# A two-layer trunk on one core: square root of the last norm on ScalarE, and a planner that counts TensorE's instruction transfers

## The chip, the cores and the metric

The kernel runs on one core of one Trainium2 chip. The metric is device time in microseconds, the median of several executions. Beside it there is one profiled execution, whose trace gives the time of every instruction; "span" is the time from its first to its last instruction.

## The reference

The kernel computes a trunk of two layers on x (1 x 256 x 1024, float32) with 256 memory tokens. Every layer is a SwiGLU block, a mixer with memory cross-attention beside it, and a second SwiGLU block, each behind a residual and a layer norm:

```python
for i in range(DEPTH):
    x = layer_norm(ALPHA * x + 0.5 * swiglu(x, ffn1_w_gate[i], ffn1_w_up[i], ffn1_w_down[i]), ...)
    ...
    heads = jnp.concatenate([mix, memory_attention(mq, mem_k, mem_v)], axis=-1)
    x = layer_norm(ALPHA * x + heads @ w_out[i], ...)
    x = layer_norm(ALPHA * x + 0.5 * swiglu(x, ffn2_w_gate[i], ffn2_w_up[i], ffn2_w_down[i]), ...)
```

with `swiglu(x) = (silu(x @ w_gate) * (x @ w_up)) @ w_down`, widths 1024 to 2816 to 1024. Layer 0's mixer is an RWKV-7 recurrence over 12 heads of 64, layer 1's is stick-breaking attention. The layer norm is

```python
return ((xf - mu) * lax.rsqrt(var + LN_EPS) * g + b).astype(x.dtype)
```

## The kernel before, in words

The 256 rows of x are two halves of 128 partitions. All weights are streamed from HBM once, in blocks (tiles `raw`), mainly over SP's queue, some issued from ScalarE. For most large products a weight block is split by ScalarE and VectorE into a rounded part (`hi`) and the rest (`lo`); x and the hidden activations (`hT`) are split the same way, and TensorE multiplies hi by hi, lo by hi and hi by lo in f32r, three 128x512 matmuls where native float32 would take one in two passes. Some blocks are multiplied unsplit in native float32 (`raw` as an operand of a matmul). Layer 0's recurrence is worked in chunks of 64 rows, as many small 64x64 products in native float32 (the tiles `Y`, `T`, `Tt`, `Lm`, `L`, `S`, `vn`, `Sk`, `kn`, `qr` in the rows below); each of these stands as two matmuls in the trace. These small products fall around 250 to 285 us and 400 to 430 us, between large products of the projections, which fill the waits of the recurrence. `ps_N` are banks of PSUM.

The order of the work is not that of the code. The class `Plan` records every operation as an `Op` with its engine and what it depends on (`add`), gives it a duration by shape (`price`), and plays a list scheduler over the five engines (`order`): at each step the free operation with the best urgency is placed, buffers of a tag and, where an operation may run on either ScalarE or VectorE, its engine are chosen, and the model keeps account of semaphores, table loads of ScalarE (`SETS` lists the functions that share a table) and TensorE's clock window (`WINDOW`). `improve` takes each operation's urgency from `URGENCY`, a packed table of numbers, one for each operation in the order of recording. `issue` then writes out all instructions in that order, so that every instruction has one and the same line in the profile: L767 before, L788 after the change. Each engine runs its own instructions strictly in the written order.

`layer_norm` computes one half's norm on VectorE: the residual is added, then bn_stats and bn_aggr give mean and variance (`mv[:, 0:2]`), a `tensor_scalar` gives −(var + eps)/2 in `mv[:, 3:4]`, and `rsqrt` finds the inverse root in `mv[:, 2:3]` from an integer shift (a second `tensor_scalar`) and three Newton rounds of two `scalar_tensor_tensor` each, with a scratch tile of the tag `nw`. Every piece of x then takes two operations, one that subtracts the mean and multiplies by g, and one that multiplies by the inverse root and adds b. `closing` is set for the very last norm of the program (half 1 of layer 1), which works in pieces of 512, 256 and 256 columns; behind each piece its output DMA is issued.

Of the kernel before, what the change touches and what calls it, by code (L numbers as in the profile page):

```python
# [23 lines left out]
P = 128  # L24
# [48 lines left out]
FLAGS = dict(t1=False, bt=False, dc=False, out1=False, zl2=False, pb=False, xt=False, mn=False, tn=False, vn=False)  # L73
# [40 lines left out]
class Op:  # L114
    __slots__ = ("i", "eng", "calls", "took", "lag", "after", "opens", "closes", "pri", "func", "port", "left", "ready",
                 "end", "users", "kb", "turns", "mode", "share", "spent", "fine", "parts", "round", "places", "ways")


class Engine_:
# [7 lines left out]
SETS = (("Exp", "Tanh"), ("Sigmoid", "Tanh"), ("Ln",), ("Silu", "Tanh"))  # L127
# [3 lines left out]
WINDOW = 3413.0  # L131
ROUNDS = 50
# [3 lines left out]
    'c-l?edDu=>)Iad^B%+Y1P)Q;s6=fbmL?lCo43#-UGDb2Kp(0~4&lJi~B2qFWDnq778YLo%l9KT3-)Fz~dtLAEkLS9Fv(MgZeb;w=*V^Zt`>FG32;'  # L136
    'DOz$(YPZa^&9-K1@rJwg3C~|G)2T%nwPDq@4=kY488JDoO72I{vaGS$!#lSw8>i^Wncjc;RFS<DGLbYwGxd%abIhV<&%4ec$EkBzfF-YySMd&yV@'
    'M>W|dtZaGq)i<eE3Hm5^qa7~hY^Gygl%(wHu5PsSjLeq>%@`%4B=5K%b|GnPl-0=rO$bLnVJj$mf{vI&r4Q#x^_+8Q03nBFLdg|^ZnXxZ~D&~FPy'
    'p^&f$$78y&W5n!$|PwEk3xBq<jo@?{Cb=D92?D^`>#)uedpP=J!S8j>`9XGVhH!1PJMpTeE*p1bN=OL)2(cqb8C_m>6#>4#)i-?6KwBHlD*Dpx+R'
    '3~*j(!S5H{YJBp>}6!rb%_?sWb;=6VON$NV*b`-JPv!=9;ZZ^Q0~ehZ-)zw+IXBu)4<%wHz{KE<}K#&luFmDV0mAW1s?9K!C0lVtPc5OTIjl6qf+'  # L140
    'aBN2i#lE)weMvI^E-`*Jgu*qG<X+zuGXJ^GN%CO9B>CIt*R5S;eF%95C&`{gA!IbZ>=HH^b2WRHR!fp~FNKh+gn3ql@b^t{5%2fl*u4}VHiR&ft('
    'Eg6NkOkWDksU)+fw+nHtxdBNm3u)bIak)<`AZx3*ldLjgLGy9KsP;oq$`lTax5qz8vkFB-eEb;T9OoESV(3jk^MdpRwz&A8`;C2R6dmoa<npOi7Z'
    '=14H-)Kd-KuBoE<M^O+(1$*-&458=h8NwT<QlH^(zLT>ym3e!LLgs>e)3KU9`x$@-6{7G_|c(tx0SIk-as}MSe5a$0A!rfvu@}m%Lo5{ZEAzTZ$o'
    'P4O`c*8OL+MFbHCx)=<l_c4=B7_c;tb<2Oe=!zUbK%_ZoJo=oFLsqrk`go0lDqn3LzpvR!M$lohQ8_Hs%@9T)-t#wo@W{)N!E(|U!Nqimxr(%*D~'
    '?tCpdI1oFu<-dBQVEGS=FgaNtMW-Ebm=+u?JHALWaMFyxxFWHOFyY!pISb7sZk_V_dMSO`7X{rR;?GV0MJx#!yu?!t$XzI%m@C1BH<&)<G0M&fwh'
    'Yj!a_$DgCK#T>uxy@zgy*%{oaAO>y4bU&WFg>z5do+KUK;YYO)t{01U#J6}a`68}oa6POJ;SDj(^(LQ=hA_i=@6v#Q@}o7shv3<Pen~QJaR{eimz'
    '7QBehOg<9Z3_%+ed{^>Q#Il7s4~n&CRD~rITb6j0>I#VH;oH!L2dIt*hwxt`H`Rc{8!T*Vrn?mYW2??df4aWBOs8p13g@*Oz&pzLHK_r`^Nwe>O>'
# [140 lines left out]
class Plan:  # L288
# [217 lines left out]
    def order(self, given=()):  # L506
# [1386 lines left out]
```

## Time and profile before

| | us |
|---|---|
| median of 3 executions | 1061.63 (1060.88 to 1062.44) |
| the profiled execution | 1061.31 |
| its span | 1059.5 |
| mean clock granted to TensorE | 0.994 of full speed |
| TensorE busy | 1041.7 |
| VectorE busy | 883.6 |
| ScalarE busy | 740.9 |

How it is read: PE is TensorE, PEld its weight loads, DVE VectorE, ACT ScalarE, POOL GpSimd and SP SyncE. A list of waits puts each idle time of an engine down to the operation that came last among those awaited; "issue" stands where nothing that the profile shows was awaited. A row of a timeline is start, duration, engine, line, operation, output<-inputs, tile sizes, count, and in brackets the idle time ahead of it. A row of a table of stretches is the stretch, its length, the busy time (and instruction count) of PE, PEld, DVE, ACT and POOL, TensorE's granted clock, the DMA engines' share and GB/s. Buffer numbers in names tell which buffer of a tag the operation got.

### The profile page before, as it was taken

What the parts mean: (1) busy time and instruction counts of PE and PEld (TensorE: products, weight loads), DVE (VectorE), ACT (ScalarE), POOL (GpSimd) and SP (SyncE); (2) the same over time, 40 slices, a digit from 0 to 9 for tenths busy, and PEclk for the clock granted to TensorE, in tenths of its full rate; (3) what the DMA queues carried; (4) which work ended last, traced back from release to release, by engine and by line L of the source; (5) the groups of instructions that cost most, each with busy time, mean ns of one, the idle gap of its engine ahead of it and who ended that gap; (6) DMA issues with size and microseconds to landing.
All of it is one profiled execution on the core that took longest, in us unless ns stands there. A gap on an engine that the chain in (4) does not pass through costs nothing.

```text
span 1059.5 us, 17849 instructions
## 1 busy us (share of the span) xinstructions
PE 1041.7 (98%) x6275; PEld 835.5 (79%) x6275; DVE 883.6 (83%) x1241; ACT 740.9 (70%) x1065; POOL 5.3 (0%) x20
## 2 busy tenths in 40 slices
PE   9999999999899999999999999999999999999996
PEld 7888888877688776688888888888778777878885
DVE  6676679999899997898799755469899999976688
ACT  6665559968689887667677544457987998865572
POOL 0000000000000000000000000000000000000000
PEclk9999999999899999999999999999999999999998
DMA  9997869779399788799899966677989989997891
GB/s 327 329 369 242 270 215 352 247 253 336 115 338 328 255 264 290 242 339 329 284 340 366 325 211 215 193 255 254 370 297 313 364 285 304 368 349 258 276 311 67
DMA packets 212684, 303.19 MB, mean 286 GB/s; under 512 B 13892, under 2 KB 159728, under 8 KB 212594
## 3 DMA queue, kind: packets, MB, share of 16 engines
q1 hardware_dynamic: 212050, 301.53, 85.5%
q8 instruction: 49, 0.80, 0.3%
q10 hardware_dynamic: 544, 0.52, 0.2%
q14 instruction: 41, 0.34, 0.1%
HBM read 300.95 MB, written 1.05 MB: 285 GB/s over the span
## 4 chain that ended last, share of the span: by engine, by line
PE 97%; DVE 1%; ACT 1%; DMA 0%; issue 0%; SPq 0%; DVEq 0%; ACTq 0%
PE ps_29r L767 30%; PE ps_30r L767 28%; PE ps_27r L767 8%; PE ps_26r L767 8%; PE ps_3r L767 8%; PE ps_25r L767 8%; PE ps_5r L767 4%; PE ps_6r L767 3%; DMA raw_12r<-in_ffn_w_up_dram 0%; DVE x L767 0%; DVE L_345r L767 0%; SPq L767 0%; ACT hi_10r L767 0%; ACT Lm_333r L767 0%; DVE lo_11r L767 0%
## 5 line engine op out<-in xcount | busy, mean ns | idle before, releaser
L767 PE MATMUL ps_29r<-hi_13r,xTh 128*128 128x512 f32 x64 | 26.3, 411 | 0.0
L767 PE MATMUL ps_29r<-hi_43r,xTh 128*128 128x512 f32 x64 | 26.0, 406 | 0.0
L767 PE MATMUL ps_29r<-lo_14r,xTh 128*128 128x512 f32 x66 | 25.8, 390 | 0.0
L767 ACT ACTIVATE idle_2r<-ps_29r 128x256 f32<-128x256 f32 (+1 forms) x31 | 12.8, 411 | 18.4 <-PE ps_29r L767 18.3
L767 PE MATMUL ps_29r<-hi_46r,xTh 128*128 128x512 f32 x62 | 25.1, 405 | 0.0
L767 PE MATMUL ps_29r<-hi_43r,xTl 128*128 128x512 f32 x64 | 25.1, 392 | 0.0
L767 PE MATMUL ps_29r<-hi_13r,xTl 128*128 128x512 f32 x64 | 25.0, 391 | 0.0
L767 PE MATMUL ps_29r<-hi_46r,xTl 128*128 128x512 f32 x62 | 24.2, 390 | 0.0
L767 PE MATMUL ps_29r<-lo_44r,xTh 128*128 128x512 f32 (+1 forms) x62 | 23.8, 383 | 0.0
L767 PE MATMUL ps_30r<-lo_11r,xTh 128*128 128x512 f32 (+1 forms) x62 | 23.8, 383 | 0.0
L767 PE MATMUL ps_29r<-lo_11r,xTh 128*128 128x512 f32 x58 | 22.8, 392 | 0.7 <-DVE lo_11r L767 0.7
L767 PE MATMUL ps_30r<-hi_46r,xTh 128*128 128x512 f32 (+1 forms) x58 | 23.0, 396 | 0.0
L767 PE MATMUL ps_29r<-hi_7r,xTh 128*128 128x512 f32 x54 | 22.6, 419 | 0.1
L767 PE MATMUL ps_30r<-lo_17r,xTh 128*128 128x512 f32 x58 | 22.6, 390 | 0.0
L767 PE MATMUL ps_29r<-lo_8r,xTh 128*128 128x512 f32 x58 | 22.6, 390 | 0.0
L767 PE MATMUL ps_29r<-lo_17r,xTh 128*128 128x512 f32 x58 | 22.6, 390 | 0.0
L767 PE MATMUL ps_30r<-lo_47r,xTh 128*128 128x512 f32 x58 | 22.6, 390 | 0.0
L767 PE MATMUL ps_30r<-hi_46r,xTl 128*128 128x512 f32 (+1 forms) x58 | 22.2, 383 | 0.0
L767 PE MATMUL ps_30r<-hi_22r,xTh 128*128 128x512 f32 x54 | 22.1, 410 | 0.0
L767 PE MATMUL ps_29r<-hi_16r,xTh 128*128 128x512 f32 x54 | 22.1, 409 | 0.0
L767 PE MATMUL ps_30r<-hi_10r,xTh 128*128 128x512 f32 x54 | 22.1, 409 | 0.0
L767 PE MATMUL ps_29r<-lo_47r,xTh 128*128 128x512 f32 x56 | 21.8, 390 | 0.0
(2125 smaller groups left out, 3922.4 us busy)
## 6 DMA issues: line engine op xcount, KB each, us to landing
raw_21r<-in_ffn_w_down_dram SPq DMA_DIRECT2D x19, 512.0 KB, 5.4
raw_67r<-in_ffn_w_gate_dram SPq DMA_DIRECT2D x32, 256.0 KB, 5.8
raw_67r<-in_ffn_w_up_dram SPq DMA_DIRECT2D x32, 256.0 KB, 6.0
raw_15r<-in_ffn_w_down_dram SPq DMA_DIRECT2D x16, 512.0 KB, 6.0
raw_12r<-in_ffn_w_gate_dram SPq DMA_DIRECT2D x31, 256.0 KB, 4.0
raw_12r<-in_ffn_w_up_dram SPq DMA_DIRECT2D x31, 256.0 KB, 4.6
raw_45r<-in_ffn_w_gate_dram SPq DMA_DIRECT2D x31, 256.0 KB, 6.3
raw_45r<-in_ffn_w_up_dram SPq DMA_DIRECT2D x31, 256.0 KB, 5.5
```

The source lines that it names most:

```text
L767: fn(*[at(x) for x in a], **{n: at(x) for n, x in k.items()})
```

## The change

It has three parts. `price` counts TensorE's instructions of each operation, and `order` moves a position `issued` along TensorE's instruction stream; where it crosses an edge (the first at 94.7, then every 127.1 counted matmuls) less than 5500 ns after the last crossing, the scheduler's model adds the difference to the operation's modelled time. `URGENCY` is replaced by another table (the old one without, the new one with these edges). And the closing norm takes its inverse root another way: a first square root of a constant, due behind the last silu, stands for the load of the table; a second one takes sqrt(var + eps) on ScalarE; VectorE takes its reciprocal and one Newton round (`polish`).

```diff
-FLAGS = dict(..., vn=False)
+FLAGS = dict(..., vn=False, sq=True)
...
-SETS = (("Exp", "Tanh"), ("Sigmoid", "Tanh"), ("Ln",), ("Silu", "Tanh"))
+SETS = (("Exp", "Tanh"), ("Sigmoid", "Tanh"), ("Ln",), ("Silu", "Tanh"), ("Sqrt",))
...
+FETCH = 5500.0
+CHUNK = 127.1
+CHUNK0 = 94.7
...
 URGENCY = (
...
@@ price
+            o.count += 1 if method == "transpose" or st.dtype == F32R else 2
...
@@ order
+        issued, edge, crossed = 0, CHUNK0, -FETCH
...
+                first, took_, stall = issued, took, 0.0
+                issued += o.count
+                while issued > edge:
+                    at_ = t + stall + took_ * (edge - first) / o.count
+                    if at_ < crossed + FETCH:
+                        stall += crossed + FETCH - at_
+                        at_ = crossed + FETCH
+                    crossed = at_
+                    edge += CHUNK
+                took = took_ + stall
...
+    def polish(dst, a, t):
+
+        nc.vector.scalar_tensor_tensor(t, dst, dst, a, ALU.mult, ALU.mult)
+        nc.vector.scalar_tensor_tensor(dst, t, 1.5, dst, ALU.add, ALU.mult)
...
@@ layer_norm
-        rsqrt(mv[:, 2:3], mv[:, 3:4], 1)
+        if FLAGS["sq"] and closing:
+            sd = new(tp_, [P, NH], F32, "nw", "sd", 2)
+            first = nc.scalar.activation(sd[:, 1:2], ident[:, :1], AF.Sqrt)
+            first.after.append(max(o.i for o in nc.ops if o.func in ("Silu", "Tanh")))
+            nc.scalar.activation(sd[:, :1], mv[:, 3:4], AF.Sqrt, scale=-2.0)
+            nc.vector.reciprocal(mv[:, 2:3], sd[:, :1])
+            polish(mv[:, 2:3], mv[:, 3:4], sd[:, 2:3])
+        else:
+            rsqrt(mv[:, 2:3], mv[:, 3:4], 1)
```

The new table moves operations on all engines by a few places; the number of TensorE's rows (4592) stays. Three places are shown as the order has them, before and after, without row numbers.

The first is TensorE in the first stretch of small products of the recurrence: three groups of 24 products (Y·T, T·Y and Tt·Lm) with large 128x512 products around them. Before:

```order
L767 MATMUL ps_30r<-hi_22r,lo_11r 128x512
L767 MATMUL ps_29r<-hi_40r,hi_7r 128x512
L767 MATMUL ps_29r<-lo_41r,hi_7r 128x512
L767 MATMUL ps_29r<-hi_40r,lo_47r 128x512
L767 MATMUL ps_26r<-Y_340r,T_339r 64x64 x2
...
L767 MATMUL ps_25r<-T_339r,Y_340r 64x64 x2
...
L767 MATMUL ps_26r<-Tt_332r,Lm_333r 64x64 x2
...
L767 MATMUL ps_29r<-hi_16r,hi_7r 128x512
```

After:

```order
L788 MATMUL ps_29r<-hi_65r,lo_11r 128x512
L788 MATMUL ps_25r<-Y_340r,T_339r 64x64 x2
...
L788 MATMUL ps_26r<-T_339r,Y_340r 64x64 x2
...
L788 MATMUL ps_29r<-hi_40r,hi_46r 128x512
L788 MATMUL ps_29r<-lo_8r,hi_46r 128x512
L788 MATMUL ps_29r<-hi_40r,lo_11r 128x512
L788 MATMUL ps_29r<-hi_40r,hi_46r 128x512
L788 MATMUL ps_29r<-lo_8r,hi_46r 128x512
L788 MATMUL ps_29r<-hi_40r,lo_11r 128x512
L788 MATMUL ps_25r<-Tt_332r,Lm_333r 64x64 x2
```

Each shortened run is 12 rows of the same kind, over two banks by turns. Six large products now stand between the second group and the third, where none stood before.

The second is TensorE in the second stretch, around the products L·Tt and vn·Sk of a later chunk. Before:

```order
L767 MATMUL ps_5r<-S_113r,qr_377r 64x64 x2
L767 MATMUL ps_3r<-vn_314r,Sk_344r 64x64 x2
L767 MATMUL ps_27r<-vn_314r,Sk_344r 64x64 x2
...
L767 MATMUL ps_26r<-raw_48r,hT_945r 128x512
L767 MATMUL ps_6r<-L_345r,Tt_332r 64x64
L767 MATMUL ps_5r<-L_345r,Tt_332r 64x64
```

After:

```order
L788 MATMUL ps_5r<-S_113r,qr_377r 64x64 x2
L788 MATMUL ps_26r<-raw_51r,hT_945r 128x512
L788 MATMUL ps_29r<-hi_49r,xTh 128x512
L788 MATMUL ps_29r<-lo_41r,xTh 128x512
L788 MATMUL ps_29r<-hi_49r,xTl 128x512
...
L788 MATMUL ps_5r<-L_345r,Tt_332r 64x64
...
L788 MATMUL ps_3r<-vn_314r,Sk_344r 64x64 x2
L788 MATMUL ps_27r<-vn_314r,Sk_344r 64x64 x2
```

The 12 rows of vn·Sk moved behind the group L·Tt, and six large f32r products (two triples) stand ahead of that group.

The third is VectorE at the end of the program: the closing norm, x_79 being half 1 of x, mv its statistics, nw the scratch tile, raw_45 and raw_42 (after: raw_67 and raw_70) g and b. Before:

```order
L767 BN_AGGR mv_574r<-st_573r 128x2
L767 TENSOR_SCALAR mv_574r<-mv_574r 128x1 x2
L767 SCALAR_TENSOR_TENSOR nw_381r<-mv_574r 128x1
L767 SCALAR_TENSOR_TENSOR mv_574r<-nw_381r,mv_574r 128x1
L767 SCALAR_TENSOR_TENSOR x_79<-x_79,mv_574r,raw_45r 128x256
L767 SCALAR_TENSOR_TENSOR nw_381r<-mv_574r 128x1
L767 SCALAR_TENSOR_TENSOR x_79<-x_79,mv_574r,raw_45r 128x512
L767 SCALAR_TENSOR_TENSOR mv_574r<-nw_381r,mv_574r 128x1
L767 SCALAR_TENSOR_TENSOR x_79<-x_79,mv_574r,raw_45r 128x256
...
L767 SCALAR_TENSOR_TENSOR x_79<-x_79,mv_574r,raw_42r 128x512
L767 SCALAR_TENSOR_TENSOR x_79<-x_79,mv_574r,raw_42r 128x256 x2
```

After:

```order
L788 BN_AGGR mv_574r<-st_573r 128x2
L788 TENSOR_SCALAR mv_574r<-mv_574r 128x1
L788 SCALAR_TENSOR_TENSOR x_79<-x_79,mv_574r,raw_67r 128x512
L788 RECIPROCAL mv_574r<-nw_288r 128x1
L788 SCALAR_TENSOR_TENSOR nw_288r<-mv_574r 128x1
L788 SCALAR_TENSOR_TENSOR mv_574r<-nw_288r,mv_574r 128x1
L788 SCALAR_TENSOR_TENSOR x_79<-x_79,mv_574r,raw_67r 128x256
L788 SCALAR_TENSOR_TENSOR x_79<-x_79,mv_574r,raw_70r 128x512
L788 SCALAR_TENSOR_TENSOR x_79<-x_79,mv_574r,raw_67r 128x256
L788 SCALAR_TENSOR_TENSOR x_79<-x_79,mv_574r,raw_70r 128x256 x2
```

And ScalarE's last rows after the change (before, they end with the hT copy):

```order
L788 ACTIVATE idle_1r<-ps_29r 128x256
L788 ACT_TABLE_LOAD
L788 ACTIVATE nw_288r<-cst 128x1
L788 ACTIVATE hT_1954r<-ps_6r 128x256
L788 ACTIVATE nw_288r<-mv_574r 128x1
```

Seven small operations of `rsqrt` left VectorE and three came; the 512-wide piece that needs only the mean stands between the square root's input and the reciprocal; a table load and two small square roots came to ScalarE, the load ahead of the last copy of `hT`.

More of the change, by code (lines that the diff above doesn't have):

```diff
@@ L115 @@
     __slots__ = ("i", "eng", "calls", "took", "lag", "after", "opens", "closes", "pri", "func", "port", "left", "ready",
-                 "end", "users", "kb", "turns", "mode", "share", "spent", "fine", "parts", "round", "places", "ways")
+                 "end", "users", "kb", "turns", "mode", "share", "spent", "fine", "parts", "round", "places", "ways", "count")
 class Engine_:
@@ new lines @@
+    '2TG8YJVH!(>FWh!59nrIb9)ye|N>$rd$Xmt^M)t7|WFop{cmCxc-49neiUa7DA14F>XGW`8b!yd;W{Dte9@I+{>QZw<v_JBSYx9C>=Ky3*q@ELMZ'
+    'xFjJvCZutUD;&h+|(7{7G3`}V|m>D3`DbJj9qc=_WPH{KdT!8~&4JZI$bdgr-PEzbWE<42uBSo3#`n^wk{z9NKS_N*7x#C2a^A41JCav`>5kB9Jk'
+    '+ZY#j58=v>V*I{r2%is%@tbQy7@-!goQW}iC9yi^DCd8%d<fS%%T3nVF2)sp3RDlFlCxc2G=z(<3L$ri5OVg7@f~qiliM4fjxn29N)-wr|H&A0T6'
+    'e`maxIS!Hwodn4QjbQ#z&tCVaAuP^ZZn2*f%+ZLXXDy+vpIAf2Iz8w@~+D;;1Nw=-RPzxaF-F8~+sJyy+nfNQw8|7!URg;W0T~>8uxOsntX3Cy%+'
+    'lk8y;!a@BF})9_R}#yQW&c%+8&zYXhm!%poG%J+zIbgvLPu2=f)F~0Cvj9+~i<6o^pxLfUOIM4TEVyq^A1=RA3>q59r9_wA33I!I*iSxX4PYA^d+'
@@ new lines @@
+    'wbmFsO{cdex8G+*{5SXaf@DZO`!+Hup-7iax?FS5WdV2W6|9q{AKN1+J}(6jI-FIhd#J5BO?@8k~`e>>YwrM3aPNOcskBcrT<SK6nid&()wc4Jux'
+    'ml7Q)}lVti21n>B|MxNqc4kHX8579lLZS^n#VFkNj6sl`s`IaAHKPNd^2rBmVXzj8iMzF@lL+8B4~rTZI(Q2ogeIt+{PX8<mx*1y~z<LhnU4^FRX'
+    'DZcz6xGc1mkN<v)u|%5~v&iuSS=2mxD*UQncER@eIWbO3$5_krH%<wm@_f1d2WA(9(0>TLT5}8>9~uzCp*Lb2G&qET{oNz>#baaKB7dtEIm2IK7#'
+    '`zn*Z*)+jO*rwaI@!MUn3s5p3)rN9<g^<^{%d7W98nujel0#M!0C2{#CO9^1fBR#;t{!zti#D+i(Z7<3EqF^cx|dfcS&6uDw1LhMZ5w?)v>hn6Kb'
+    '$-S?;COn90zTTN%B!tEE*@mGCx6Py-Q-%?+OFcGfmi=&FT#<UKhOScfF>Vt7JV;m`;ch?MIkep?mV$W;TXj2Fe&VtGPF}{qS3c~YfoHSgWs=g-wZ'
@@ new lines @@
+    '^7Ro_u_=Yui{>Lx+QBWZ2u!2d+Mvn_<NP}UDFQ+#6L;Sc2y1GQ#F6OMU3l<!@70vJC%-CKB}h9-&;R*EdhJhDsTV7xbS6!aqK(seGtM-N%&;4T09'
+    'oQ{K_FL?4n0&$JnBGD&$`i;|#qr?|n7;i8lO|j`v(CrVsSXeXcDSLR<B?AcpdAGZQCGfd8w+T0^h2uN%Vme$Ny0P3~>|JFKZu3D<1KJ0Gjx2bZVg'
+    'A9}OGarin8BOR^PEQE5MV;nNqHH}lDuo{-b7ro&ji#{DQFdh5;7D5v>p3y%Q=H3-!Q*q^8mX6zZ(WZ7G%!2O{a<TIzJmlV_*SpY^=k(meUfT&zv-'
+    ';sPI=Esr9MFemU#Vxy5T2?Z!dcj@lkmR&>@mZ>8F&j%O~ogm61zLsr}}aVT)q7b{N)H?Bd+|g2_C+HSMlU1{Cz@gf2TS3;MF}-L%4jN`oewDYhr9'
+    'Gwtg^QOOM<RFB|uzW1~G8Ve|*-SXYnFnPgwQw@IJg>h-E>)T>pDZ^`42@X=^pjQ{*Egs*Y)KxZu@)^_T(N*&(&I>!G-dAuitcm7Mq9l28B**v&Q4'
@@ new lines @@
+    '^&pGtn{bTelbr>$BcL6`{NMqxWrnkLwL7wI<8o(xBf>9^!A>LFh`Hp*|WQTObwUwg7S-tf02_s;wubOEk^Jat7v^T{joX5;>&R;JpU<<ulm3vt^b'
+    '*3w<-xEH|d{RF^-XwT&rkIkq}PPuKn-DxWQ|CXw52|T8Iw4qNh&E?>2o=QS6r_7}C4V9uV*07)$#5o-bnTrj~nQex|%1_IEM$UaF?^)b>{W*HUfD'
+    'rS&z_Fnj?nv`>52Wx@GF^y~pV*vEb|JomYp?S;!?F!_k{T|=XDKN#a-d8#>5&0zWoxzB*pEIsrBeteBbDbX<<*Yg6)pGbw>xaKSSEpCz#E|#~3*3'
+    'I`%2;1|fV|F#nhcDW?r{rK7h<gu+^96je<TY9?-nVv$uNd4~@AYl+DYjnn(s5smH{1WhuQ7Ip#fE&?MDg9PM(=p8jh>(C_a}ZXJc85Q_Y`jaPhaG'
+    'w1=U_mg+2{jcWsQvXW>}+y_0A7-0RD6$jh*n8^;!q*VXiEt{V2%UmIv_S3aUV>}+;zSDtSGY-GhtO=<9Peq@?hZ-(_6xbz1(IjI&^X!yJQz%KezQ'
@@ new lines @@
+    'QzOxAQj%9o{rrTznS2w0zTRv!YKE5mxJT-^aee-4vtsBbYA<vej|TkuZQ@DM59J~?ppfypBT=l&*AgxmuQc33>W89uvk)GU%54ePFvIQWqSM#4PA'
+    'qC>frdp@LCdnYg=P7++QVEd7Lq8Ovfj0OodbWdp7>=Xa7d{Y6wkT!=t_FT;=HJ&Gf5)ntdqVoUW<u9F3cX@G7p{fLqr(%k$QqQaFT)@b#1WUGM(u'
+    'oULoZvud`<<F$Ax>;3XB<|3D-LW!$m+&Z0C?1CG`KRMxcIsFXIzQPHst<^xkKgs{pg8du$le8ZFT<m-G#ltU%_Z2yjYtkB5$y+Dd_^IoDp?f(l<r'
+    '&p#|DQ3oE)~M=#JkGD`||d+bxwA~{}aRwLl4O5R5{%&$HV;oSS=4`&s_U1K5{UBa*3Ya;<?3JV@&Gs&lS!DzZ>=Qd-UN~eKyqI6RkDK9-a7-lHwU'
+    ')uM7767KbMNS4f|=(~ouJ?WkHjr1xLY@2&K6K3w*;TxU4n65em2czzZCy>gq~bJuL)4dLbY?lD&C9Kug9yJ`}ylamMF^-ncA4CAG7<XCa-rg<CG^'
@@ L475, in price @@
             fun = a[2] if len(a) > 2 else k["func"]
-            o.func = {AF.Exp: "Exp", AF.Tanh: "Tanh", AF.Sigmoid: "Sigmoid", AF.Ln: "Ln", AF.Silu: "Silu"}.get(fun)
+            o.func = {AF.Exp: "Exp", AF.Tanh: "Tanh", AF.Sigmoid: "Sigmoid", AF.Ln: "Ln", AF.Silu: "Silu", AF.Sqrt: "Sqrt"}.get(fun)
             ptr = sum(isinstance(k.get(x), bass.AP) for x in ("scale", "bias"))
```

277 lines of the change are left out of this document (129 added, 148 removed).

## The prediction

> **What bounds the kernel now.** I read the page first: the busy line, the transfers of instructions, and the chain of work that ended last by engine.
>
> ```profile
> PE 1041.7 (98%) x6275; PEld 835.5 (79%) x6275; DVE 883.6 (83%) x1241; ACT 740.9 (70%) x1065; POOL 5.3 (0%) x20
> q8 instruction: 49, 0.80, 0.3%
> PE 97%; DVE 1%; ACT 1%; DMA 0%; issue 0%; SPq 0%; DVEq 0%; ACTq 0%
> ```
>
> TensorE is busy in 1041.7 of 1059.5 us, and the chain is TensorE's for 97%. So a change that leaves the matmuls as they are can win only in TensorE's waits, in its clock, and in what follows the last matmul. The second view is therefore the list of TensorE's waits, by releaser: total, times, longest.
>
> ```profile
> PE ps_6r L767 <- issue: 2.0, 2, 1.4
> PE ps_6r L767 <- DVE L_345r L767: 1.7, 1, 1.7
> PE ps_3r L767 <- POOL lastc L767: 1.0, 1, 1.0
> PE ps_5r L767 <- ACT Lm_333r L767: 0.7, 1, 0.7
> PE ps_29r L767 <- DVE lo_11r L767: 0.7, 1, 0.7
> PE ps_5r L767 <- DVE S_113r L767: 0.7, 1, 0.7
> PE ps_5r L767 <- DVE L_345r L767: 0.6, 1, 0.6
> PE ps_6r L767 <- DMA x<-in_x_dram: 0.6, 1, 0.6
> PE ps_5r L767 <- ACT memKT L767: 0.6, 1, 0.6
> ```
>
> These nine are 8.6 us; the rest is smaller. The largest entry, 2.0 us in two waits, has no releaser at all ("issue"). The timeline shows where the two stand:
>
> ```profile
> 257.11 0.28 PE L767 MATMUL ps_26r<-Tt_332r,Lm_333r 64*64 64x64 f32 x3
> 258.06 0.21 PE L767 MATMUL ps_6r<-Tt_332r,Lm_333r 64*64 64x64 f32 x1 [0.67 <-issue]
> ...
> 416.80 0.22 PE L767 MATMUL ps_5r<-L_345r,Tt_332r 64*64 64x64 f32 x1
> 418.38 0.21 PE L767 MATMUL ps_6r<-L_345r,Tt_332r 64*64 64x64 f32 x1 [1.36 <-issue]
> ```
>
> Each is in the midst of a group of equal 64x64 products whose operands are the same tiles before and behind the gap, so no tile is awaited. The table of stretches counts matmuls and gives TensorE's clock (PEclk, 1.00 is full) and each engine's busy time:
>
> ```profile
> 258.05:418.30 160.25, 155.25 (x1654) 120.00 (x1654) 147.04 (x249) 129.81 (x225) 2.61 (x7) 0.98 0.80 266
> 255.00:283.00 28.00, 23.67 (x589) 19.24 (x589) 21.95 (x39) 19.06 (x39) 1.40 (x4) 0.88 0.64 213
> 283.00:400.00 117.00, 117.00 (x751) 92.21 (x748) 113.52 (x197) 99.46 (x168) 0.95 (x2) 1.00 0.83 276
> 400.00:430.00 30.00, 28.00 (x624) 18.55 (x622) 22.31 (x30) 20.69 (x33) 0.26 (x1) 1.00 0.83 267
> ```
>
> Between the two waits lie 1654 matmuls. The page has 6275 matmuls and as many weight loads on 49 transfers of 0.80 MB: about 256 instructions, 128 matmuls, a transfer. 1654 is 12.9 of these, nearly a whole number. I read both waits as TensorE running out of instructions at a transfer's edge, in the two stretches where matmuls are so short that 128 of them take about 6 us (28.00/589 and 30.00/624, times 128), not the 20 us of 283 to 400 (117.00/751).
>
> **The change part by part.** *The planner's counting.* No engine gets other matmuls; rows on TensorE shift by 3.3 places on average. What counts is how long TensorE is kept busy between one edge and the next:
>
> ```profile
> 252.61:257.39 4.78, 4.78 (x124) 3.92 (x115) 4.32 (x9) 4.48 (x8) 0.26 (x1) 1.00 1.05 383
> 411.99:416.98 4.99, 4.99 (x128) 3.38 (x128) 3.21 (x6) 4.15 (x7) 0.00 (x0) 1.00 0.98 332
> 402.37:407.04 4.67, 4.67 (x150) 3.59 (x149) 3.86 (x6) 4.38 (x7) 0.00 (x0) 1.00 0.87 244
> ...
> 1045.84 2.04 PE ps_3r L767 x9
> ```
>
> The first two rows are the shares of one transfer that run dry: 4.78 us of work and 0.67 of wait (5.45 from edge to edge), 4.99 and 1.36 (6.35). A 128x512 f32r product costs 2.04/9 = 0.23 us. In the new order the share ahead of the first edge holds three more such products for three short ones (about 0.02 us each): 4.78 + 3 × 0.23 − 0.06 = 5.4 us, 0.05 short of 5.45. Ahead of the second, the 24 short vn·Sk products (48 matmuls, two passes each) move behind the group and six 512-wide f32r products come in; counting 127 matmuls back from the group, at this trace's durations, I get 7.2 us, more than 6.35. Neither group then waits, and no other share falls under 5.0. So 2.0 us go; bounds: nothing (both waits move elsewhere) to −2.0. I take −2.0, near the end that the two intervals give. The third row is a warning: a share of 4.67 us passed without a wait, so the interval needed isn't constant.
>
> *What is late next.* The chain of the recurrence behind 258 is in the same order on TensorE and VectorE, so the waits on L, Lm and S (1.7, 0.7, 0.7, 0.6) stay. In 283 to 400 TensorE waits for nothing, and VectorE is busy 113.52 of 117.00 us. Near 390 the new order has five copies moved from ScalarE to VectorE and two moved back, net three pieces about as large as 128x256: 1.4 us at the 0.48 of such a piece (rows below). It has 3.48 us of slack; I cost this at nothing, hidden by that slack, and at up to +1.4 if it is not. SP's and POOL's queues have the same number of entries, and only x at the start keeps TensorE waiting on a DMA (0.6): nothing is costed for loads.
>
> *The last norm.* Its VectorE rows now, and ScalarE's that price the new operations:
>
> ```profile
> 1052.17 0.34 DVE L767 TENSOR_SCALAR mv_574r<-mv_574r 128x1 f32<-128x1 f32 x2
> 1052.55 0.22 DVE L767 SCALAR_TENSOR_TENSOR nw_381r<-mv_574r 128x1 f32<-128x1 f32 x1
> 1052.81 0.16 DVE L767 SCALAR_TENSOR_TENSOR mv_574r<-nw_381r,mv_574r 128x1 f32<-128x1 f32 x1
> 1052.88 0.48 DVE L767 SCALAR_TENSOR_TENSOR x<-x,mv_574r,raw_45r 128x256 f32<-128x256 f32 x1
> 1053.28 0.21 DVE L767 SCALAR_TENSOR_TENSOR nw_381r<-mv_574r 128x1 f32<-128x1 f32 x1
> 1053.41 0.75 DVE L767 SCALAR_TENSOR_TENSOR x<-x,mv_574r,raw_45r 128x512 f32<-128x512 f32 x1
> 1054.07 0.15 DVE L767 SCALAR_TENSOR_TENSOR mv_574r<-nw_381r,mv_574r 128x1 f32<-128x1 f32 x1
> ...
> 1054.98 1.54 DVE L767 SCALAR_TENSOR_TENSOR x<-x,mv_574r,raw_42r 128x512 f32<-128x512 f32 x3
> ...
> 3.04 0.20 ACT L767 ACTIVATE idle_2r<-idle_1r 128x1 f32<-128x1 f32 x1
> 274.89 0.17 DVE L767 RECIPROCAL rs_606r<-rs_606r 128x2 f32<-128x2 f32 x1
> 274.96 0.47 ACT L767 ACTIVATE idle_1r<-ps_27r,rs_606r 128x256 f32<-128x256 f32 x1 [0.46 <-DVE rs_606r L767]
> 1044.97 0.39 ACT L767 ACTIVATE hT_2024r<-ps_5r 128x256 fp32r<-128x256 f32 x1 [2.36 <-PE ps_27r L767]
> L767 ACT ACT_TABLE_LOAD x15 | 19.2, 1283 | 2.2 <-issue 1.7 <-PE ps_29r L767 0.2
> ```
>
> From the start of TENSOR_SCALAR to the end of the last piece it is 1052.17 to 1056.52, 4.35 us, for three Newton rounds with the mean's subtractions as filling. Afterwards, in steps from start to start as the rows give them: TENSOR_SCALAR to an independent piece 0.13 (as 1053.28 to 1053.41), the 512 piece 0.66 (1053.41 to 1054.07), RECIPROCAL 0.23 (0.17 and a gap), the round's first half 0.26, its second 0.07, a 256 piece 0.40 (1052.88 to 1053.28), the 512 apply 0.70 (between 0.66 and its own 0.75), then three 256 pieces 0.40, 0.40, 0.39. Sum 3.64: 0.7 saved. I take −0.65, since the trace has no step out of such a RECIPROCAL.
>
> The change adds a wait there: RECIPROCAL for ScalarE's square root, with the round, five pieces of x and the output queued behind it. TENSOR_SCALAR's first half ends at 1052.34, the hop to ScalarE is about 0.1 (a reciprocal from 274.89 for 0.17, consumer at 274.96), a 128x1 ACTIVATE 0.20, a hop back: done near 1052.7, while the 512 piece keeps VectorE until 1052.96. Were it as dear as the 0.47 of the 128x256 row, it would still just fit. The table load (1.28) and the first, idle square root (0.20) wait for the last silu and stand ahead of the hT copy at 1044.97, which TensorE's last products need; they take 1.48 of 2.36 us idle there. Without that room the load would cost up to 1.28 less what VectorE covers, 1.0 us: bounds −0.9 to +0.3.
>
> **Sum**, against the profiled execution's 1061.31 us (span 1059.5 and 1.8 around it; the median shown is 1061.63): 1061.31 − 2.0 − 0.65 = **1058.7**.
>
> [...]
>
> **The rivals.**
> *B: the 2.0 us are not won.* Either the instruction waits aren't of this kind or move to other shares, or the three added copies take the time back in the stretch where VectorE is 97% busy. For it: the 4.67 us share without a wait, and that 1.4 of the gain is only 1.4 of slack away. Against it: the 1654. Time: 1061.31 − 0.65 = 1060.7.
>
> *C: a half-clock stretch goes.*
>
> ```profile
> 274.70:281.70 7.00, 5.62 (x121) 4.97 (x117) 3.93 (x11) 4.41 (x12) 0.67 (x3) 0.51 0.17 43
> 271.30:274.80 3.50, 1.78 (x72) 1.40 (x70) 3.21 (x6) 1.88 (x6) 0.05 (x1) 1.00 0.33 123
> 415.50:418.90 3.40, 2.04 (x27) 1.12 (x27) 2.32 (x3) 1.30 (x3) 0.00 (x0) 1.00 0.99 321
> ```
>
> TensorE ran at half clock for about 7 us, a loss of 28.00 × (1 − 0.88) = 3.4, behind 3.50 us in which it stood idle for 1.72. If the moved edges or another phase of that window lessen the idle time, 3.4 more go: 1055.3. Against it: the waits that make it are kept.
>
> *D, the other side: a new half-clock stretch.* In the third row TensorE idled 1.36 of 3.40 us and the clock stayed full. If the new order has one place where it idles between 1.36 and 1.72 of 3.4 us (from there it decides), in 400 to 430 or where VectorE is full, the price is about 1.7 for the wait and 3.4 for the clock: 1058.7 + 5.1 = 1063.8.
>
> *E: the tail doesn't do what it says*, the square root coming late by what was saved: 1061.31 − 2.0 = 1059.3.
>
> **How the numbers follow.** Forecast 0.45 (1057.4 to 1059.6), B 0.25, C 0.13, D 0.14, E 0.03. A measurement of this kernel can tell about 0.2%, 2.1 us, from no change: faster is below 1059.5, slower above 1063.75. Faster: 0.42 of the forecast's 0.45 and C, 0.55. Same: the rest of it, B, E and a little of D, 0.32. Slower: 0.13. The range 1055.2 to 1062.8 takes in C's point, B and both terms' bounds, and leaves out most of D and half of C, under 2 in 10.
>
> **What would show it.** Right: no wait on "issue" in TensorE's list, the groups at 257 and 417 unbroken; the last apply ending 3.6 to 3.7 us after the last TENSOR_SCALAR starts, with RECIPROCAL not waiting for ScalarE; the table load inside idle time ahead of the last hT copy. Wrong: an "issue" wait at another multiple of 127 matmuls (B), new TensorE waits on VectorE tiles in 283 to 430 (B or D), PEclk under or over 0.88 in 255 to 283 (C), a second dip elsewhere (D).

## The result and the profile after

The changed kernel took 1056.76 us (median of 6, 1055.67 to 1058.20) against 1060.85 us (median of 6, 1059.21 to 1062.44) for the kernel before: a ratio of 0.9962 (95% interval 0.9950 to 0.9973), 4.1 us. The two profiled executions are 1058.20 and 1061.31 us, 3.1 us apart; 1058.20 is the slowest of its six.

TensorE's waits in the changed kernel, largest first, in the columns of before (total, times, longest):

```profile
PE ps_6r L788 <- DVE L_345r L788: 1.8, 2, 1.2
PE ps_3r L788 <- POOL lastc L788: 1.0, 1, 1.0
PE ps_29r L788 <- DVE lo_11r L788: 0.8, 1, 0.8
PE ps_5r L788 <- DVE S_113r L788: 0.6, 1, 0.6
PE ps_5r L788 <- ACT Lm_333r L788: 0.6, 1, 0.6
PE ps_6r L788 <- DMA x<-in_x_dram: 0.6, 1, 0.6
PE ps_6r L788 <- ACT memKT L788: 0.5, 1, 0.5
```

No "issue" is left; the waits of the recurrence on L, S, Lm and memKT are there as before, with nearly the sizes of before. The stretches, in the columns of before:

```profile
255.00:283.00 28.00, 24.82 (x547) 19.69 (x543) 22.38 (x40) 19.33 (x40) 1.40 (x4) 0.88 0.63 222
283.00:400.00 117.00, 116.97 (x790) 91.51 (x787) 113.22 (x199) 97.88 (x165) 0.95 (x2) 1.00 0.82 276
400.00:430.00 30.00, 29.40 (x604) 19.96 (x594) 23.68 (x32) 21.21 (x36) 0.26 (x1) 1.00 0.82 271
```

TensorE is busy 24.82 instead of 23.67 us in the first stretch and 29.40 instead of 28.00 in the last; in between VectorE stays at 113 of 117 us and TensorE still waits for nothing. The clock in the first stretch is 0.88 again: that half-clock stretch is in both profiled executions.

The end of the program on VectorE and ScalarE:

```profile
1049.97 0.15 DVE L788 TENSOR_SCALAR mv_574r<-mv_574r 128x1 f32<-128x1 f32 x1
1050.04 0.74 DVE L788 SCALAR_TENSOR_TENSOR x<-x,mv_574r,raw_67r 128x512 f32<-128x512 f32 x1
1050.70 0.15 DVE L788 RECIPROCAL mv_574r<-nw_288r 128x1 f32<-128x1 f32 x1
1050.89 0.22 DVE L788 SCALAR_TENSOR_TENSOR nw_288r<-mv_574r 128x1 f32<-128x1 f32 x1
1051.14 0.16 DVE L788 SCALAR_TENSOR_TENSOR mv_574r<-nw_288r,mv_574r 128x1 f32<-128x1 f32 x1
1051.22 0.48 DVE L788 SCALAR_TENSOR_TENSOR x<-x,mv_574r,raw_67r 128x256 f32<-128x256 f32 x1
...
1052.67 0.88 DVE L788 SCALAR_TENSOR_TENSOR x<-x,mv_574r,raw_70r 128x256 f32<-128x256 f32 x2
...
1040.41 1.28 ACT L788 ACT_TABLE_LOAD   x1
1041.70 0.20 ACT L788 ACTIVATE nw_288r<-cst 128x1 f32<-128x1 f32 x1
1042.75 0.38 ACT L788 ACTIVATE hT_1954r<-ps_6r 128x256 fp32r<-128x256 f32 x1 [0.84 <-PE ps_3r L788]
1050.16 0.20 ACT L788 ACTIVATE nw_288r<-mv_574r 128x1 f32<-128x1 f32 x1 [7.03 <-DVE mv_574r L788]
```

From the start of TENSOR_SCALAR to the end of the last piece it is 1049.97 to 1053.55, 3.58 us, where it was 4.35. The square root ends at 1050.36 and RECIPROCAL comes at 1050.70 without a wait. The span ends 2.85 us behind the last piece, before 2.98.

So the 3.1 us of the profiled pair are these: the last matmul ends at 1048.47 instead of 1050.67 (2.2 us), and what follows it takes 7.93 instead of 8.83 us (0.9). The medians are 1 us further apart than this pair, and that is what the experiments had to find beside the causes.

### The profile page after: what moved, and what is told of

Its sections match the earlier page's. It is cut to its first block, busy times and chain, and to the rows that moved or that the text cites. A ratio compares the mean times of both kernels' runs of the same rounds, so it can differ in the third digit from the quotient of the medians.

```text
span 1056.4 us, 17846 instructions
## 1 busy us (share of the span) xinstructions
PE 1041.8 (99%) x6275; PEld 835.8 (79%) x6275; DVE 886.2 (84%) x1241; ACT 741.6 (70%) x1064; POOL 5.3 (0%) x20
## 4 chain that ended last, share of the span: by engine, by line
PE 95%; DMA 2%; DVE 1%; ACT 1%; issue 0%; SPq 0%; DVEq 0%; ACTq 0%
PE ps_30r L788 28%; PE ps_29r L788 27%; PE ps_26r L788 8%; PE ps_3r L788 8%; PE ps_27r L788 8%; PE ps_25r L788 8%; PE ps_5r L788 3%; PE ps_6r L788 3%; DMA raw_9r<-in_ffn_w_down_dram 1%; DMA raw_18r<-in_ffn_w_up_dram 1%; DMA raw_48r<-in_ffn_w_up_dram 1%; DMA raw_12r<-in_ffn_w_up_dram 1%; DVE x L788 0%; DVE L_345r L788 0%; DVE lo_47r L788 0%
## 5 line engine op out<-in xcount | busy, mean ns | idle before, releaser
L788 PE MATMUL ps_29r<-lo_11r,xTh 128*128 128x512 f32 (+1 forms) x64 | 24.6, 385 | 0.8 <-DVE lo_11r L788 0.8
L788 PE MATMUL ps_30r<-lo_11r,xTh 128*128 128x512 f32 x64 | 25.0, 390 | 0.0
L788 PE MATMUL ps_30r<-lo_8r,xTh 128*128 128x512 f32 x62 | 24.2, 391 | 0.0
L788 PE MATMUL ps_30r<-hi_10r,xTl 128*128 128x512 f32 x60 | 23.5, 392 | 0.0
L788 PE MATMUL ps_30r<-lo_14r,xTh 128*128 128x512 f32 x60 | 23.4, 390 | 0.0
L788 PE MATMUL ps_29r<-hi_65r,xTh 128*128 128x512 f32 x56 | 22.8, 407 | 0.0
L788 PE MATMUL ps_29r<-lo_47r,xTh 128*128 128x512 f32 (+1 forms) x58 | 22.2, 383 | 0.0
L788 PE MATMUL ps_30r<-hi_7r,xTh 128*128 128x512 f32 (+1 forms) x56 | 21.9, 392 | 0.0
L788 PE MATMUL ps_29r<-hi_65r,xTl 128*128 128x512 f32 x56 | 21.9, 392 | 0.0
L788 PE MATMUL ps_30r<-lo_41r,xTh 128*128 128x512 f32 x56 | 21.9, 390 | 0.0
```

What stands on the lines that cost most here:

```text
L788: fn(*[at(x) for x in a], **{n: at(x) for n, x in k.items()})
```

## The experiments

The theory: the two parts add, the planner's part wins because TensorE runs dry at the edges of its instruction transfers, and the new order keeps those edges out of the short products. The rivals: the order gains otherwise; the waits belong to those products whatever the edges; most of the gain is the tail's.

**The two parts alone.** `replan` is the changed kernel with the old inverse root, `tail` the kernel before with the new one; in each the last urgencies are the other kernel's, so that nothing else moves. The edit of `replan`, without its table:

```diff
-FLAGS = dict(..., vn=False, sq=True)
+FLAGS = dict(..., vn=False, sq=False)
```

> The changed kernel with the closing norm's inverse root as before (integer shift and three Newton rounds on VectorE), and the new order otherwise. The prediction's theory: the two parts add; here only the waits for instructions are won, so this run has no wait on 'issue' in TensorE's list, its last matmul ends about 2.2 us earlier than before, and from the last residual add to the end it takes about 9.5 us as before: profiled about 1059.1, against before about -2.2 us (ratio 0.998). Rival, the new order gains by something else and the waits for instructions cost nothing: then the gain is also here, but the stretches 255 to 283 and 400 to 430 take as long as before. Rival, the tail makes most of the 4.1 us of the medians: then this run is within 1 us of the kernel before.

> The kernel before with the closing norm's inverse root as in the changed kernel, the old order elsewhere. The prediction's theory: both waits on 'issue' stay at their places (0.7 and 1.4 us), the last residual add to the end takes 8.6 us instead of 9.5: about -0.9 us (ratio 0.9992). Rival, the tail makes most of the 4.1 us of the medians: then -2 us or more here.

`replan`: 1057.84 against 1060.88 us, ratio 0.9972 (0.9963 to 0.9981), 3.0 us, with no "issue" wait. Its profiled execution took 1056.87 us where 1059.1 was expected: it lacks the half-clock stretch (clock 1.00 in 255 to 283, where the changed kernel has 0.88). `tail`: 1060.12 against 1060.88, ratio 0.9994 (0.9982 to 1.0006): too small to be told from nothing in the medians, but its trace has TENSOR_SCALAR at 1051.29 and the last piece's end at 1054.87, 3.58 us, as in the changed kernel. 3.0 and 0.8 make up the 4.1 within their intervals: the parts add, and the tail is the smaller one. Unexpected was `tail`'s list of waits, whose order on TensorE is that of before:

```profile
PE ps_6r L762 <- issue: 2.8, 2, 1.4
PE ps_6r L762 <- DVE L_345r L762: 1.7, 1, 1.7
PE ps_3r L762 <- POOL lastc L762: 1.0, 1, 1.0
PE ps_5r L762 <- issue: 0.9, 1, 0.9
```

Three waits at edges, 3.7 us in all, not 2.0 in two; the clock in 255 to 283 was 1.00 here too.

**Moving the edges.** In `before_shift96` and `after_shift96` the order is untouched, but 114 small matmuls take the place of the first 18 instructions, so that all later ones stand 96 places further on in the stream.

```diff
+                    if getattr(o, "again", 0):
+                        a = (a[0][:32, :16], a[1][:, :32], a[2][:, :16])
+                    for _ in range(getattr(o, "again", 0) or 1):
+                        fn(*[at(x) for x in a], **{n: at(x) for n, x in k.items()})
...
     warm(WARM[0])
+    for j, o in enumerate([o for o in nc.ops if o.eng == "PE"]):
+        o.again = 57 * (j + 1) // 9 - 57 * j // 9
```

> The kernel before in the same order, with the first nine matmuls on an idle tile (18 instructions of 128 columns) replaced by 114 of 16 columns: every later matmul stands 96 places further on in the instruction stream, and the edges of the transfers fall 96 matmuls earlier in the program. Transfers theory: the waits follow the count. The shares that run dry are now one of 2.8 us of work ending 31 matmuls behind the old first wait (at about 258.5 of the old clock) and one of 2.5 us ending at about 406.4; an edge takes 5.5 to 6.4 us to the next, so waits of about 2.6 to 3.6 and 3 to 4 us there, none in the group L*Tt at 417; if such a wait brings a half-clock stretch, 3.4 us more for each. Sum: 4 to 5 us slower, with half clock up to 12 us slower. Rival, the waits belong to those products or to a fixed moment: 0.7 and 1.4 us at the same matmuls, time unchanged but for a start later by up to 2 us.

> The changed kernel with the same displacement of 96 matmuls. Transfers theory: the new order fits the old edges only, so the waits come back: shares of 4.2 us (ending near 258.5) and 3.2 us (ending near 406.2) run dry, waits of 1.3 to 2.2 and 2.3 to 3.2 us, 4 to 5 us slower than the changed kernel, with half-clock stretches up to 12. Rival, the new order is better in itself, whatever the edges: no wait on 'issue', time as the changed kernel but for a start later by up to 2 us.

`before_shift128` and `after_shift128`, with 73 in place of 57, displace by 128, a whole transfer, and are the control.

> The kernel before with 146 small matmuls of 16 columns in place of the first 18 instructions: every later matmul stands 128 places further on, one whole transfer. A control for the displacement by 96. Transfers theory: the edges fall on the same products as in the kernel before, so the waits on 'issue' are back inside Tt*Lm at the first place and inside L*Tt (417 us of the old clock) at the second, 2 to 4 us in all, two to three waits; time above before by the later start alone, about 2 us. Rival, the small matmuls at the start or the later start move the waits: they stand elsewhere or are gone.

> The changed kernel with the same displacement by a whole transfer. Transfers theory: no wait on 'issue', time above the changed kernel by the later start alone, about 2 us (1058.5 to 1059.5), where the displacement by 96 cost 3.8. Rival, the small matmuls cost this by themselves: 1060.7 or more, as with 96.

The waits without a releaser, in the timelines of `before_shift96` (three rows), `before_shift128` (three rows) and `after_shift96` (one row); `after_shift128` has none:

```profile
261.74 0.21 PE L770 MATMUL ps_6r<-Tt_332r,Lm_333r 64*64 64x64 f32 x1 [2.20 <-issue]
410.86 0.59 PE L770 MATMUL ps_26r<-raw_9r,hT_945r 128*128 128x512 f32 x1 [0.97 <-issue]
424.00 0.21 PE L770 MATMUL ps_6r<-vn_314r,kn_313r 64*64 64x64 f32 x1 [0.77 <-issue]
```

```profile
261.94 0.21 PE L770 MATMUL ps_6r<-Tt_332r,Lm_333r 64*64 64x64 f32 x1 [1.22 <-issue]
416.33 0.21 PE L770 MATMUL ps_5r<-vn_314r,Sk_344r 64*64 64x64 f32 x1 [0.56 <-issue]
422.52 0.21 PE L770 MATMUL ps_6r<-L_345r,Tt_332r 64*64 64x64 f32 x1 [1.08 <-issue]
```

```profile
261.50 0.27 PE L791 MATMUL ps_5r<-Tt_332r,Lm_333r 64*64 64x64 f32 x2 [1.20 <-issue]
```

How many matmuls had started ahead of each is read from the table of stretches, cut just ahead of the wait. The first two rows are of before, then the runs in the order just given, one fence each:

```profile
0.00:258.05 258.05, 254.76 (x1494) 206.17 (x1495) 204.66 (x297) 178.16 (x274) 2.65 (x13) 1.00 0.89 294
0.00:418.37 418.37, 410.01 (x3148) 326.17 (x3149) 351.70 (x544) 307.98 (x499) 5.27 (x20) 0.99 0.85 284
```

```profile
0.00:261.73 261.73, 258.55 (x1622) 210.81 (x1623) 206.90 (x299) 178.02 (x274) 2.65 (x13) 1.00 0.88 292
0.00:410.85 410.85, 402.89 (x3021) 324.16 (x3022) 343.51 (x535) 302.31 (x490) 5.41 (x20) 0.99 0.85 280
0.00:423.99 423.99, 415.27 (x3276) 331.88 (x3277) 353.27 (x545) 310.14 (x502) 5.41 (x20) 0.99 0.85 281
```

```profile
0.00:261.93 261.93, 259.53 (x1622) 211.68 (x1623) 205.14 (x298) 177.43 (x274) 2.66 (x13) 1.00 0.88 291
0.00:416.32 416.32, 409.59 (x3148) 328.15 (x3149) 347.60 (x539) 303.42 (x492) 5.38 (x20) 0.99 0.85 280
0.00:422.51 422.51, 414.70 (x3276) 331.61 (x3277) 351.63 (x544) 307.56 (x499) 5.38 (x20) 0.99 0.85 281
```

```profile
0.00:261.49 261.49, 258.21 (x1620) 210.07 (x1621) 208.35 (x299) 179.10 (x274) 2.65 (x13) 1.00 0.88 291
```

Whatever product stands there, a wait comes at the count 1494, 1620 or 1622, 3020 or 3021, 3148 or 3276: 1494 plus 1, 12, 13 and 14 steps of 127 or 128. Displaced by 96, it hits other products, or in the group Tt·Lm one 32 matmuls further on (1622 less 96 is 1526); displaced by 128, it is back at those of before (1622 less 128 is 1494, 3148 less 128 is 3020, 3276 less 128 is 3148; 3020 is where `tail` had its third wait), and the changed kernel, clear of it at 0 and at 128, meets it at 96 (1620). That speaks against the rival that ties the waits to the products.

The instruction queue in the view of DMAs shows the cause directly. Narrowed to a few microseconds, that view has a single transfer on queue q8 ahead of each wait: in the kernel before from 255.59 to 256.70 us for the wait that ends at 258.06, and from 416.01 to 416.95 for the one that ends at 418.38. Over all 14 waits on "issue" in these runs, `tail` and `before_again`, the first matmul behind the wait starts 1.2 to 1.6 us after a transfer has landed. The size of a wait thus follows from when its transfer starts: at the first place, 3.2 us behind the edge before it in the kernel before (a wait of 0.7 us), 3.9 in `tail` (1.4) and 4.0 in `before_again` (1.4). Why the start varies no run shows.

The sizes were forecast too large. `before_shift96` had 2.2, 1.0 and 0.8 us where about 3 and 3 to 4 were expected, `after_shift96` 1.2 us and nothing at the second place. The medians are 1063.71 against 1060.88 (ratio 1.0023, 1.0009 to 1.0037), 1064.01 against 1061.08 for `before_shift128` (1.0026, 1.0015 to 1.0037), 1060.73 against 1060.88 for `after_shift96` (0.9997, 0.9985 to 1.0009) and 1060.36 against 1061.08 for `after_shift128` (0.9990, 0.9978 to 1.0002). The later start has to be taken off. The idle matmul behind the replaced ones, at 6.7 us in both kernels, starts at 8.9 with 96 and at 10.7 us with 128, but part of that goes into the wait of 0.6 us for x, which the displaced runs of the kernel before no longer have: behind 1400 matmuls (1496 and 1528 in the displaced runs) they are 1.7 and 3.3 us late. For 128 about 2 us was expected, and so `after_shift128` missed its 1058.5 to 1059.5; in the medians alone it stands nearer to the rival's 1060.7. With 1.7 and 3.3 us taken off, the displacement by 96 costs the changed kernel 3.9 − 0.2 − 1.7 = 2.0 us (3.9 is its gain in its own second run, below), that by 128 nothing (3.9 − 0.7 − 3.3 = −0.1). For the kernel before, which has such waits undisplaced too, the same sums are 1.1 and −0.4; these are estimates, since the runs are of different jobs.

Both orders displaced by 96 are still 3.0 us apart (1060.73 and 1063.71; some 0.9 of it is the tail's), though neither was planned for those edges. That fits the waits, 1.2 us in the one and 3.9 in the other, but it also means that most of the gain doesn't hang on the edges being where the planner has them.

**Both kernels once more.**

> The changed kernel once more, beside the kernel before on the same chip. Transfers theory with the half clock as a second, chance part: no wait on 'issue' again, median 3.5 to 4.5 us below before, and the executions' granted clock in a narrower band than before's (0.995 and up, before 0.991 to 0.998). Rival, the 4.1 us of the first medians were partly chance: the median difference comes out at 2.7 to 3.1, the sum of the profiled pair.

> The kernel before once more, one look. If the wait at a transfer's edge is always of the same size, the two waits on 'issue' are 0.7 and 1.4 us again. If it varies with when the transfer starts, as the run with the tail alone suggests (1.4, 0.9 and 1.4 us at the edges, in the same order of TensorE), the waits stand at the same matmuls, or at another edge of the same stretches, with other sizes, 2 to 4 us in all. Half clock in 270 to 285 present or absent by chance.

`after_again`: 1056.97 against 1060.90 us, ratio 0.9964 (0.9951 to 0.9976), 3.9 us, so the 4.1 were not chance; no "issue" wait. `before_again` has these, and this clock in 270 to 285 and 405 to 430:

```profile
PE ps_6r L767 <- issue: 3.3, 2, 1.9
...
258.92 0.21 PE L767 MATMUL ps_6r<-Tt_332r,Lm_333r 64*64 64x64 f32 x1 [1.37 <-issue]
417.84 0.21 PE L767 MATMUL ps_6r<-L_345r,Tt_332r 64*64 64x64 f32 x1 [1.91 <-issue]
...
270.00:285.00 15.00, 11.78 (x310) 9.89 (x304) 12.56 (x33) 9.83 (x24) 0.80 (x3) 1.00 0.31 105
405.00:430.00 25.00, 22.52 (x454) 15.03 (x448) 17.35 (x23) 14.67 (x24) 0.00 (x0) 0.93 0.76 249
```

The same program, the same two matmuls, 3.3 us instead of 2.0. And in the second stretch, around a wait of 1.91 us, the clock lost 25.00 × (1 − 0.93) = 1.75 us, where it was full (1.00) in the first profile; in 270 to 285 it was full (1.00), as in `tail`. `after_again` shows 0.77 in 270 to 285 and 1.00 in 405 to 430:

```profile
270.00:285.00 15.00, 12.34 (x217) 10.28 (x218) 11.26 (x30) 8.66 (x22) 0.67 (x3) 0.77 0.21 73
405.00:430.00 25.00, 24.40 (x447) 15.90 (x440) 20.22 (x28) 17.01 (x28) 0.00 (x0) 1.00 0.83 276
```

The granted clock of the executions of that job lies between 0.991 and 0.998 for the kernel before (25 of them, 0.9946 on average) and between 0.995 and 0.997 for the changed one (10, 0.9961). The narrower band isn't certain: the ten of `no_polish`, below, lie between 0.993 and 0.998. Executions at the same clock can be compared: at 0.995 the kernel before averages 1060.0 us (5 executions) and the changed one 1057.5 (2), at 0.996 it is 1059.8 (3) and 1057.1 (5). So 2.5 to 2.7 of the 3.9 us are there at equal clock, and by this estimate some 1.2 us goes with the clock.

**The planner's count without effect.** The table is replayed, but the stall is never added.

```diff
-FETCH = 5500.0
+FETCH = 0.0
```

> The changed kernel with FETCH at 0, so that the planner replays the same table without the added stalls; TensorE's order is then the same up to about 402 us and differs behind. If the table alone carries the gain: no wait on 'issue', median within 1 us of the changed kernel. If the counted stalls decide the order in the second stretch: a wait on 'issue' of 1 to 2 us, or new waits on VectorE's tiles, between 400 and 430 us, and a median 1 to 3 us above the changed kernel.

1060.34 against 1061.08 us, ratio 0.9999 (0.9989 to 1.0010): the gain is gone, though neither branch describes it. There is no "issue" wait in its profiled execution, but there are new waits on tiles, mostly ScalarE's, at 438 to 456 us, behind the stretch that was named:

```profile
PE ps_27r L788 <- ACT xTh L788: 0.7, 1, 0.7
PE ps_26r L788 <- ACT hT_1042r L788: 0.5, 1, 0.5
PE ps_5r L788 <- DVE Y_340r L788: 0.3, 1, 0.3
```

The table holds urgencies, not an order; replayed under another model of time it gives another order, not the one it was made for. So this run does not measure what counting is worth. The three waits are 1.5 us; with the gain of `after_again` the changed kernel would stand at 1057.2 in this job, 3.2 us below. Where the rest went isn't shown.

**The table's load and the Newton round.** `no_preload` leaves out the idle square root that stands for the load: it stays in the plan, so that the order is the same, but isn't written out. `no_polish` leaves the Newton round out, and its two numbers of the table.

```diff
-                for fn, a, k in o.calls:
+                for fn, a, k in () if getattr(o, "mute", False) else o.calls:
...
             first = nc.scalar.activation(sd[:, 1:2], ident[:, :1], AF.Sqrt)
+            first.mute = True
```

> The changed kernel without the first, idle square root: the table load then stands directly ahead of the real square root, behind the last hT copy. If the load runs as soon as ScalarE comes to it, it falls into the 7 us in which ScalarE waits for VectorE's statistics: no change (within 0.1 us). If it waits with the square root: the square root ends 1.28 us later, at 1.7 us behind the end of TENSOR_SCALAR's start, RECIPROCAL waits about 1.0 us for ScalarE, and the end is 1.0 us later.

```diff
-            polish(mv[:, 2:3], mv[:, 3:4], sd[:, 2:3])
```

> The changed kernel without the Newton round behind the reciprocal (the inverse root is then as exact as ScalarE's square root and VectorE's reciprocal make it). RECIPROCAL to the next piece of x falls from 0.52 us to 0.1: the end comes 0.4 us earlier than in the changed kernel, 4.0 to 4.8 us below before in the medians.

`no_preload`: 1057.21 against 1060.90, ratio 0.9964 (0.9951 to 0.9977), that of the changed kernel. Its ScalarE rows:

```profile
1041.69 0.38 ACT L788 ACTIVATE hT_1954r<-ps_6r 128x256 fp32r<-128x256 f32 x1 [2.35 <-PE ps_3r L788]
1042.09 1.28 ACT L788 ACT_TABLE_LOAD   x1
1049.08 0.20 ACT L788 ACTIVATE nw_288r<-mv_574r 128x1 f32<-128x1 f32 x1 [5.70 <-DVE mv_574r L788]
```

The load runs as soon as ScalarE comes to it, 5.70 us ahead of the square root, and not with the wait of the square root. Loading ahead is thus right, but the idle square root isn't what brings it about.

`no_polish`: 1056.67 against 1060.90, ratio 0.9962 (0.9950 to 0.9974). RECIPROCAL to the next piece is 1049.34 to 1049.42, 0.08 us instead of 0.52, as expected, and TENSOR_SCALAR to the last piece's end 1048.61 to 1051.74, 3.13 us instead of 3.58. The medians of the changed kernel in the same job are 0.3 us above it: not told apart by the intervals.

## Why the prediction was right, and where its size was off

- *The two waits are TensorE running out of instructions at a transfer's edge*: right. The displaced orders and the landings 1.2 to 1.6 us ahead of each wait's end show it; the count 1654 between them was the sign that mattered.
- *The new order leaves no share short enough to wait*: right in all profiled executions of the changed kernel's whole order, with and without the tail and displaced by a whole transfer, but only just. The 127 matmuls ahead of the count 1494 took 5.9 us, and the instructions had landed 1.5 us ahead, where waits end 1.2 to 1.6 us behind a landing: nothing was to spare. (The 5.4 and 5.45 of the sum came from a row of 124 matmuls; between the counts 1367 and 1494 the kernel before has 5.0 us of work and the wait, 5.7 in all.) The second edge, at 3148, fell not in L·Tt, for which the sum had 7.2 us, but in vn·Sk right behind it, with a share of 6.4 us. And no fixed length decides: counted in the table of stretches, in the three undisplaced executions of the old order shares of 5.0 and 5.1 us of work always ended in a wait, one of 5.9 in one of three, one of 4.7 and one of 5.4 never. At most of the 49 edges TensorE did not wait for instructions; at two or three it did, with 2.0 to 3.7 us of waits in each of the four profiled executions of the old order that were not displaced by a part of a transfer.
- *"So 2.0 us go; bounds: nothing (both waits move elsewhere) to −2.0"*: this is the step that failed, by size. The median of 1056.76 lies below the 1057.4 to 1059.6 that the forecast gave itself, inside the wider range only. The 2.0 are those of one execution. The same order had 2.0, 3.7 (`tail`), 3.3 (`before_again`) and 1.2 + 0.6 + 1.1 = 2.9 us (`before_shift128`), 3.0 on average, and `replan` gained 3.0. The bound of the gain should have been above the one trace's figure. A part may also be clock, which the sum left as it was: the stretch around a wait of 1.91 us lost 1.75 us by its clock in one execution, and at equal clock the whole gain is 2.5 to 2.7 us, about the 2.65 of the sum. Against that, TensorE's idle time up to its last matmul is 9.0, 10.3 and 10.6 us in the kernel before, `before_again` and `tail`, and 6.1 to 6.8 in the five undisplaced executions of the new order (`no_count` aside), 3.5 us less on average, which leaves nothing for the clock. So whether the missing part is waits or clock stays open.
- *The tail, −0.65*: 0.9 in the profiled pair. VectorE's steps took 3.58 us where the sum had 3.64, so −0.77, where I had taken 0.65, less than the sum's 0.7; 0.13 more came behind the last piece, which the prediction did not reckon with. The hop to ScalarE, the 0.20 us square root and the cover by the 512 piece were as reckoned: done at 1050.36, needed at 1050.70.
- *The table load is hidden in ScalarE's idle time ahead of the hT copy*: right, and in `no_preload` its 1.28 us, from 1042.09, were hidden behind the copy as well.
- *The copies moved to VectorE cost nothing*: right; 283 to 400 has no TensorE wait.
- *The waits of the recurrence stay*: right, though on L they are 1.8 in two for 1.7 and 0.6, 0.5 us less. With the 2.0 that would be 2.5; the last matmul came 2.2 us earlier, so smaller waits took 0.3 back.
- *Rival C, that the half-clock stretch at 275 goes*: not decided by the order. Executions of one order show the 15 us at 0.77 and at 1.00 for before, and for the order of the changed kernel at 0.77, 0.89 (`no_preload`, `no_polish`) and 1.00 (`replan`). I had taken it for a fixture of the kernel, kept because its waits are kept; it comes and goes between executions. That a phase of some window has a part in it was a supposition; no run shows one.
- *Rival D, a new half-clock stretch*: none appeared in the changed kernel (1.00 in all stretches from 285 to 1046 us); the old order has a dip in `before_again`, 0.93 in 405 to 430, around the wait at 417. Idle time alone, as D reckoned by an estimate from two rows, doesn't decide it: around the 2.20 us wait of `before_shift96` the clock is 1.00 (250 to 270 us).

## What to carry to other kernels

A wait without a releaser in the midst of equal instructions is worth counting instructions for: where such waits are whole transfers apart, displace the stream by part of a transfer and by a whole one, and see whether they move and come back. Find the transfer that lands ahead of each wait. What one trace gives for such a wait is one draw; profile the same program two or three times before a term is made of it. A table of urgencies is only as good as the model it is replayed under.

## What the runs showed of the hardware

- Instructions came to TensorE in 49 transfers of about 256 instructions (twice 6275 over 49), each 0.9 to 1.7 us long in the kernel before. Among short matmuls, TensorE stood still at some edges for 0.6 to 2.2 us, until 1.2 to 1.6 us after a transfer had landed; such waits came at the same counts in all executions (to within two matmuls), but not at every edge each time, and for different times.
- In `no_preload` a table load of ScalarE (1.28 us) ran while the instruction behind it was still waiting for its operand, and ended 5.70 us ahead of it.
- The half-clock stretch in 270 to 285 (0.51 in 274.7 to 281.7 in the kernel before) was there or not in executions of one and the same program, with the same longest wait of 1.7 us on L in all three undisplaced executions of the old order (clock 0.77 in the kernel before, 1.00 in `tail` and `before_again`).
